# Tiles of the forgetting stage's output projection loaded piece by piece, and its residual tiles one unit ahead

## The chip, the core and the metric

The kernel runs on one core of one Trainium2 chip. The metric is the device time of one execution in microseconds; lower is better.

## The reference

One decoder layer on 1024 tokens of width 1024, in float32. What matters here is the middle of it, where two head groups are joined and projected, and the memory tokens are prepared for cross-attention:

```python
fx_out = forgetting_attention(fq, fk, fv, flf).reshape(B, S, FX_W)       # 8 heads of 64, causal, with decay
x = x + jnp.concatenate([ml_out, fx_out], axis=-1) @ w_out[l]            # ml_out: the mLSTM group, 4 heads of 128
x = x + cross_attention(rmsnorm(x, ln_x[l]), rmsnorm(mem, ln_mem[l]), w_xq[l], w_xkv[l], w_xo[l])
u = jax.nn.relu(rmsnorm(x, ln2[l]) @ w_ff1[l])
x = x + (u * u) @ w_ff2[l]
```

## The kernel before, in words

Every matrix product is taken as three products of a high and a low part (`mm3`, L182 to L184). The kernel goes through its stages one after another: input projections and mLSTM heads, forgetting attention, rest of the output projection, cross-attention, MLP. The change is in the forgetting stage.

That stage is a loop over slots. A slot (`slot`) takes one step of the softmax pipeline of forgetting attention: transposes of probabilities (L767), their cut into high and low parts (L130, L131), their product with the values (L786), scores of a later tile (L719, L720), row maximum (L726, L729), exponential (L741) and scaling on POOL (L752). Since the pipeline doesn't fill TensorE, each slot also takes a few matmul steps of other work, the filler (`filler`). The filler has 28 units in a fixed order: four groups of a key unit, a value unit and a key unit (keys and values of the memory tokens for cross-attention), then 16 output units (`out_unit(hf, n)`: half `hf` of the tokens, output tile `n`), which multiply the first five of the eight tiles of the joined heads ("mixes": four mLSTM heads and the first pair of forgetting heads) with `w_out_a`, add the residual tile x (L933), and store the sum (L934).

Inside a slot the order of each compute engine's instructions is fixed as written (`in_order`), and, from the first values on, that of the DMA issues on SP too. All DMAs are issued by SP, into one queue. So an ACT or DVE instruction of the filler that waits for a load holds back the attention work written behind it on that engine.

The filler's inputs come from memory in three ways. Its weights are loaded raw into one of two `wr` tiles (`raw_load`, L952) and cut into high and low halves on ACT (L965) and on POOL or DVE (L966), a few slots later (`cut_next`; at least `AGE` = 3 slots after the load). The mixes of one half are loaded at once by `mix_in(hf)`: `mix_load` issues two DMAs of four tiles (L850) and `mix_tile` two of one tile (L856). It is called for half 0 at the start of unit 10, and for half 1 inside `out_unit(0, 4)`. The residual tile is loaded at the start of its own unit (L925).

The outputs of key units, value units and the residual tiles use small tiles [128, 512], taken in turn by `rotate("p", "a")`: three buffers, two of tag p and one of tag a.

Of the kernel before, what the change touches and what calls it, by code (L numbers as in the profile page):

```python
# [9 lines left out]
F32 = mybir.dt.float32  # L10
F32R = mybir.dt.float32r
# [7 lines left out]
T = 1024  # L19
TH = 512  # L20
D = 1024
KT = D // P
NM = 256
MLH = 4
# [4 lines left out]
KX = 1  # L29
# [15 lines left out]
def hybrid_layer(ctx: ExitStack, tc: tile.TileContext, a: dict, out: bass.AP):  # L45
# [13 lines left out]
    def sb(tag, shape, bufs, dt=F32):  # L59
        return pool.tile(shape, dt, tag=tag, name=name(tag), bufs=bufs)  # L60

    def act(dt=F32R):
        return sb("act", [P, 8, TH], 7, dt)
# [12 lines left out]
    def z4():  # L76
        return sb("z4", [P, T + 3], 2)

    def w2(tag, n=512, dt=F32, p=P):
        return sb("r_" + tag, [P, 512], BUFS[tag], dt)[:p, :n]  # L80
# [30 lines left out]
    load = nc.sync.dma_start  # L111
# [47 lines left out]
    def rotate(*tags):  # L159

        spare[tags] = spare.get(tags, -1) + 1
        return w2(tags[spare[tags] % len(tags)])
# [23 lines left out]
    def both(pair, f):  # L186
        return f(pair[0]), f(pair[1])
# [107 lines left out]
    xs = [[t[:, k] for k in range(KT)] for t in (xa, xb)]  # L295
# [21 lines left out]
    for k in range(KT):  # L317
        if k == 2:
            load(wg_raw, a["w_gate"])
        if k % 2 == 0:  # L320
            c = slice(k % 4 * 256, k % 4 * 256 + 512)
# [39 lines left out]
    z, e, q, lf = (small[:, i:j].rearrange("p (t c) -> p t c", c=c) for i, j, c in ((0, 128, GC), (128, 224, GW), (224, 320, GW), (320, 416, GW)))  # L361
# [189 lines left out]
    mix = dram.tile([2, 2, P, KT, TH], F32, name="mix")  # L551
# [126 lines left out]
    for _ in range(2):  # L678
        t = act().rearrange("p a b -> p (a b)").rearrange("p (i c) -> p i c", i=4)
# [18 lines left out]
    def fx_step():  # L698
        if coming:
            dst, src = coming.pop(0)  # L700
            load(dst.bitcast(F32), src)
# [145 lines left out]
    def mix_load(k0, k1, hf):  # L847
        t = act().rearrange("p (e k) c -> p e k c", e=2)
        for p_ in range(2):
            load(t[:, p_, : k1 - k0].bitcast(F32), mix[hf, p_, :, k0:k1])  # L850
        return [(t[:, 0, k], t[:, 1, k]) for k in range(k1 - k0)]

    def mix_tile(k, hf):
        t = z4()[:, :T].bitcast(F32R).rearrange("p (e c) -> p e c", e=2)
        for p_ in range(2):
            load(t[:, p_].bitcast(F32), mix[hf, p_, :, k])  # L856
        return t[:, 0], t[:, 1]

    def out_proj(w_src, src, hf, sink):

        kn = len(src)
        per = w_src.shape[2] // (kn * P)
        for n in range(KT):
            if n % per == 0:
                w = both(weights(w_src[n // per], kn * per * P), lambda t: t.rearrange("p (k c) -> p k c", k=kn))
            at_ = n % per * P
            ps = mm()
            for k in range(kn):
                mm3(ps, both(w, lambda t: t[:, k, at_ : at_ + P]), src[k], k == 0, k == kn - 1)
            sink(n, hf, ps)  # L870


    late = []

    def void(_):
        return None

    def key_unit(n):
        def run(ws):
            w = both(ws[0], lambda t: t.rearrange("p (k c) -> p k c", k=KT))  # L880
            ps = mm()
            for k in range(KT):
                mm3(ps[:, :NM], both(w, lambda t: t[:, k]), (hm[:, 0, k], hm[:, 1, k]), k == 0, k == KT - 1)
                yield 1.5, k == KT - 1, lambda: sink(ps)

        def sink(ps):
            t = rotate("p", "a").rearrange("p (e c) -> p e c", e=2)
            v.tensor_tensor(out=t[:, 1], in0=ps[:, :NM], in1=row_m, op=ALU.mult)

            def store():  # L890
                split(t[:, 0].bitcast(F32R), t[:, 1].bitcast(F32R), t[:, 1])
                return lambda: void(load(kxd[n // 2, :, :, n % 2], t))

            return store

        return [a["w_xk"][n]], run

    def value_unit(hd):
        def run(ws):
            ws = [both(w, lambda t: t.rearrange("p (k c) -> p k c", k=4)) for w in ws]  # L900
            for t in range(2):
                ps = mm()[:, :NM]
                for k in range(KT):
                    x = (hm[:, 0, k, t * P : (t + 1) * P], hm[:, 1, k, t * P : (t + 1) * P])
                    mm3(ps, x, both(ws[k // 4], lambda z: z[:, k % 4]), k == 0, k == KT - 1)
                    yield 1.5, k == KT - 1, lambda: sink(t, ps)

        def sink(t, ps):
            o = rotate("p", "a").bitcast(F32R).rearrange("p (e c) -> p e c", e=2)
            split(o[:, 0], o[:, 1], ps, rcol_m[:, t : t + 1])  # L910
            return lambda: void(load(vxd[hd, :, :, t], o.bitcast(F32)))

        return [a["w_xv"][hd, i] for i in range(2)], run

    mixes = {}

    def mix_in(hf):
        mixes[hf] = mix_load(0, MLH, hf) + [mix_tile(k, hf) for k in range(MLH, MLH + KX)]

    def out_unit(hf, n):  # L920
        def run(ws):
            if n == 4 and hf == 0:
                mix_in(1)
            x = rotate("p", "a")
            load(x, a["x"][:, n, hf * TH : hf * TH + TH])  # L925
            w = both(ws[0], lambda t: t.rearrange("p (k c) -> p k c", k=MLH + KX))
            ps = mm()
            for k in range(MLH + KX):
                mm3(ps, both(w, lambda t: t[:, k]), mixes[hf][k], k == 0, k == MLH + KX - 1)
                yield 3.0, k == MLH + KX - 1, lambda: sink(x, ps)  # L930

        def sink(x, ps):
            v.tensor_tensor(out=x, in0=ps, in1=x, op=ALU.add)  # L933
            return lambda: void(load(x1d[hf, :, n], x))  # L934

        return [a["w_out_a"][n]], run

    units = []
# [45 lines left out]
    def filler():  # L984
        for u, (srcs, run) in enumerate(units):
            now[0] = u
            if u == len(units) - 2 * KT - 2:
                mix_in(0)
            while not now[2] and halves[0] < 2 * sum(w_ <= u for w_, _ in sources):
                yield None  # L990
            cut_for(u)
            yield from run(cuts_.pop(u))
# [8 lines left out]
    def slot(values, until):  # L1001
        with in_order((*COMPUTE, mybir.EngineType.SP) if values or until else COMPUTE):
            now[1] += 1
            todo_ = late[:]
            late.clear()
            closing = bool(ended)
            ended.clear()
            x = next(steps_, None) if values else None
            if x:
                x.turn()  # L1010

            while adds and not closing and len(adds) >= (LAG if x else 1):
                y = adds.pop(0)
                y.add()
                if y.last:
                    ended.append((y.hd, y.hf, y.ov))
                    break
            tops = scored[:]
            scored.clear()
            for t, e in tops:  # L1020
                t.top(e)
            if x:
                x.cut()
                adds.append(x)
            for hd, hf, ov in ended:
                fx_close(hd, hf, ov)
                if hd % 2:
                    stores.append((hd, hf, True))
            exps = topped[:]
            topped[:] = tops  # L1030
            for t, e in exps:
                t.exp(e)
            while exped:
                exped.pop(0).scale()
            exped.extend(t for t, e in exps if e == len(t.parts) - 1)
            fx_step()
            part = next(parts, None)
            if part:
                part[0].score(part[1])
                scored.append(part)  # L1040
            late.extend(filter(None, [f() for f in todo_]))
            if stores and stores[0][2]:
                stores[0] = (*stores[0][:2], False)
            elif stores:
                fx_store(*stores.pop(0)[:2])
            while spent[0] < until:
                step = next(fill, None)
                if step is None:
                    break
                spent[0] += step[0]  # L1050
                if step[1]:
                    late.append(step[2])
                    break
            if until and cut_next() and spent[0] + 6 < until:
                cut_next()
        return x
# [16 lines left out]
    n = 0  # L1073
# [4 lines left out]
    while adds or late or ended or stores:  # L1078
        n += 1
        slot(False, (n - DELAY) * RATE)  # L1080
# [233 lines left out]
    for n in range(KT):  # L1314
# [7 lines left out]
        k = n % 4  # L1322
# [128 lines left out]
    for at, (p_, i) in enumerate(jobs):  # L1451
# [14 lines left out]
        if i == 4:  # L1466
            b, k = todo[p_][:2]
# [48 lines left out]
    for at, (b, m) in enumerate(steps):  # L1516
# [10 lines left out]
        x = sums_of(m) if b == 0 else x2[m // 2][:, m % 2]  # L1527
# [22 lines left out]
    for i in range(2):  # L1550
        t = act()
# [123 lines left out]
```

## Time and profile before

| | us |
|---|---|
| median of 3 runs | 1533.2 (1532.7 to 1538.22) |
| the profiled execution's own time | 1537.44 |
| its span, first to last instruction | 1535.7 |
| TensorE matmuls busy in the span | 1504.1 |
| DVE, ACT, POOL busy | 1102.0, 731.7, 505.4 |

The time of an execution is a little longer than its span. A matmul's busy time overlaps that of the next one, so a busy TensorE is not yet one at its peak, but where it waits, the wait shows as a gap in its timeline. The forgetting stage's slots with value steps lie between about 392 and 612 us from the span's start.

### The profile page before, as it was taken

To read this page: it belongs to the slowest core of one execution; us is meant where nothing else is said; L and a number is where in the kernel's file an instruction comes from. 1 tells how busy PE (TensorE), PEld (TensorE's weight loads), DVE (VectorE), ACT (ScalarE), POOL (GpSimd) and SP (SyncE) were. 2 spreads that over 40 slices of the span, in tenths; PEclk is the share of its full clock that TensorE was granted. 3 is DMA by queue.
4 is the path that set the end of the run, shared out by engine and by line. 5 is a ranking of instruction groups with operands and counts; after the bars stand their busy time and mean duration, and the time that the engine had idled before them with its cause. 6 is when DMAs were issued, how large, how long until landed. Compare 5 with 4: busy or idle time off the path is not lost. (4 is left out here: it accounts for less than half of the span.)

```text
span 1535.7 us, 21948 instructions
## 1 busy us (share of the span) xinstructions
PE 1504.1 (98%) x7665; PEld 1260.2 (82%) x7665; DVE 1102.0 (72%) x1747; ACT 731.7 (48%) x1365; POOL 505.4 (33%) x543
## 2 busy tenths in 40 slices
PE   8999999999999999999999999999999999999997
PEld 8878888889998878788888877787787888888887
DVE  7656676764787776944557889888887567887665
ACT  7324343334686665644444457666665621121224
POOL 1002030413364442521110023554454365563322
PEclk9999999999999999999999999999999999999999
DMA  6422223435889786963344428777667777776623
GB/s 221 124 76 76 96 104 117 134 128 155 245 243 262 228 262 205 349 211 118 124 131 162 167 90 296 245 250 243 227 246 273 303 288 270 275 271 238 246 96 110
DMA packets 121530, 303.53 MB, mean 198 GB/s; under 512 B 13502, under 2 KB 28152, under 8 KB 113996
## 3 DMA queue, kind: packets, MB, share of 16 engines
q1 hardware_dynamic: 121420, 302.13, 58.2%
q8 instruction: 60, 0.98, 0.3%
q14 instruction: 50, 0.41, 0.1%
HBM read 202.22 MB, written 99.86 MB: 197 GB/s over the span
## 5 line engine op out<-in xcount | busy, mean ns | idle before, releaser
L182 PE MATMUL tp<-act,wl 128*128 128x512 f32 (+1 forms) x448 | 176.2, 393 | 1.8 <-DMA act<-mix 0.8
L183 PE MATMUL tp<-act,wh 128*128 128x512 f32 (+1 forms) x448 | 175.4, 391 | 0.0
L184 PE MATMUL tp<-act,wh 128*128 128x512 f32 (+1 forms) x448 | 175.0, 392 | 0.0
L131 DVE TENSOR_TENSOR wl<-wr,wh 128x1024 fp32r<-128x1024 f32 (+2 forms) x99 | 129.7, 1310 | 20.8 <-ACT wh L130 19.9
L130 ACT ACTIVATE wh<-wr 128x1024 fp32r<-128x1024 f32 (+2 forms) x99 | 98.9, 1000 | 84.0 <-PE tp L184 36.5
L182 PE MATMUL mm<-act,wl 128*128 128x512 f32 (+1 forms) x336 | 129.8, 386 | 0.9 <-DVE r_c L514 0.9
L183 PE MATMUL mm<-act,wh 128*128 128x512 f32 (+1 forms) x336 | 129.2, 385 | 0.0
L184 PE MATMUL mm<-act,wh 128*128 128x512 f32 (+1 forms) x336 | 128.9, 383 | 0.0
L182 PE MATMUL m<-act,wl 128*128 128x512 f32 (+1 forms) x312 | 119.7, 384 | 3.1 <-DVE wl L131 2.1
L184 PE MATMUL m<-act,wh 128*128 128x512 f32 (+1 forms) x312 | 119.7, 384 | 0.0
L183 PE MATMUL m<-act,wh 128*128 128x512 f32 (+1 forms) x312 | 119.3, 382 | 0.0
L182 PEld LDWEIGHTS tp<-act,wl 128*128 128x128 f32 x448 | 84.2, 188 | 21.7 <-ACT row L1368 1.2
L184 PEld LDWEIGHTS tp<-act,wh 128*128 128x128 f32 x448 | 84.2, 188 | 19.2
L183 PEld LDWEIGHTS tp<-act,wh 128*128 128x128 f32 x448 | 84.2, 188 | 18.9
L182 PE MATMUL sc<-act,wl 128*128 128x512 f32 (+1 forms) x248 | 97.0, 391 | 0.9 <-DVE wl L131 0.8
L183 PE MATMUL sc<-act,wh 128*128 128x512 f32 (+1 forms) x248 | 96.7, 390 | 0.0
L184 PE MATMUL sc<-act,wh 128*128 128x512 f32 (+1 forms) x248 | 96.7, 390 | 0.0
L130 ACT ACTIVATE wh<-z 128x1024 fp32r<-128x1024 f32 (+1 forms) x54 | 55.5, 1027 | 82.6 <-POOL z L1439 60.9
L1439 POOL TENSOR_TENSOR z<-wr 128x256 f32<-128x256 f32 x56 | 50.4, 921 | 133.7 <-DMA wr<-w_ff2q 126.3
L131 DVE TENSOR_TENSOR wl<-z,wh 128x1024 fp32r<-128x1024 f32 (+1 forms) x54 | 74.8, 1385 | 9.8 <-ACT wh L130 9.7
L130 ACT ACTIVATE w<-wr 128x768 fp32r<-128x768 f32 (+2 forms) x31 | 25.5, 824 | 105.0 <-PE tp L182 32.8
L182 PEld LDWEIGHTS mm<-act,wl 128*128 128x128 f32 x336 | 63.4, 189 | 13.8 <-DVE r_c L514 1.2
(683 smaller groups left out, 4254.8 us busy)
## 6 DMA issues: line engine op xcount, KB each, us to landing
act<-right SPq DMA_DIRECT2D x49, 1024.0 KB
right<-w SPq DMA_DIRECT2D x56, 256.0 KB
wr<-w_ff2q SPq DMA_DIRECT2D x28, 512.0 KB
right<-r_d SPq DMA_DIRECT2D x49, 256.0 KB
right<-r_e SPq DMA_DIRECT2D x49, 256.0 KB
act<-fqk SPq DMA_DIRECT2D x48, 256.0 KB
wr<-w_in SPq DMA_DIRECT2D x20, 512.0 KB
wr<-w_ff SPq DMA_DIRECT2D x20, 512.0 KB
```

The lines of the kernel that those rows point to most:

```text
L130: s.activation(hi, src, AF.Copy)
L131: return v.tensor_tensor(out=lo, in0=src, in1=hi.bitcast(F32), op=ALU.subtract)
L182: nc.tensor.matmul(ps, w[1], x[0], start=first, stop=False, skip_group_check=more)
L183: nc.tensor.matmul(ps, w[0], x[1], start=False, stop=False, skip_group_check=more)
L184: nc.tensor.matmul(ps, w[0], x[0], start=False, stop=last, skip_group_check=more)
L1439: g.tensor_tensor(out=o, in0=x, in1=y, op=op)
```

## The change

The mixes are no longer loaded by `mix_in` in one go. It allocates the tiles and puts ten pieces (five tiles, high and low) on a list; each slot issues one piece (`mix_step`, right behind the one load that the slot issues for the next attention head). For half 0 the list is made one unit earlier, at the start of unit 9. Whatever is left of a list is issued at the start of the first output unit of that half. Residual tiles are loaded one unit ahead (`x_in`), the first at the start of unit 11. The fillers' small tiles rotate among five buffers, `ROOM`: two of p, two of b, one of a.

```diff
-    def mix_tile(k, hf):
-        t = z4()[:, :T].bitcast(F32R).rearrange("p (e c) -> p e c", e=2)
-        for p_ in range(2):
-            load(t[:, p_].bitcast(F32), mix[hf, p_, :, k])
-        return t[:, 0], t[:, 1]
...
+    ROOM = ("p", "b", "p", "b", "a")
...
-            t = rotate("p", "a").rearrange("p (e c) -> p e c", e=2)
+            t = rotate(*ROOM).rearrange("p (e c) -> p e c", e=2)
...
     def mix_in(hf):
-        mixes[hf] = mix_load(0, MLH, hf) + [mix_tile(k, hf) for k in range(MLH, MLH + KX)]
+
+        t = act().rearrange("p (e k) c -> p e k c", e=2)
+        mixes[hf] = [(t[:, 0, k], t[:, 1, k]) for k in range(MLH)]
+        for _ in range(KX):
+            z = z4()[:, :T].bitcast(F32R).rearrange("p (e c) -> p e c", e=2)
+            mixes[hf].append((z[:, 0], z[:, 1]))
+        pieces.extend((mixes[hf][k][p_], mix[hf, p_, :, k]) for k in range(MLH + KX) for p_ in range(2))
+
+    def mix_step():
+        if pieces:
+            dst, src = pieces.pop(0)
+            load(dst.bitcast(F32), src)
+
+    def x_in(hf, n):
+        xs[hf, n] = rotate(*ROOM)
+        load(xs[hf, n], a["x"][:, n, hf * TH : hf * TH + TH])
 
     def out_unit(hf, n):
         def run(ws):
+            while n == 0 and pieces:
+                mix_step()
             if n == 4 and hf == 0:
                 mix_in(1)
-            x = rotate("p", "a")
-            load(x, a["x"][:, n, hf * TH : hf * TH + TH])
+            if hf == 0 or n + 1 < KT:
+                x_in(hf + (n + 1) // KT, (n + 1) % KT)
+            x = xs.pop((hf, n))
...
     def filler():
         for u, (srcs, run) in enumerate(units):
             now[0] = u
-            if u == len(units) - 2 * KT - 2:
+            if u == len(units) - 2 * KT - 3:
                 mix_in(0)
+            if u == len(units) - 2 * KT - 1:
+                x_in(0, 0)
...
             fx_step()
+            mix_step()
```

In the slots the compute engines keep their order: only buffer names differ there. What moves is the order on SP. Three places, each before and now. `act` and `z` with `mix` are the mixes, `fqk`, `decay` and `fvd` the next attention head's inputs, `wr` the filler's weights, `kxd` and `vxd` the stores of key and value units.

SP, around the load of half 0's mixes, up to the first weights of an output unit; before:

```order
L892 DMA kxd<-r_a_5017 256x1x256
L952 DMA wr_5096<-w_xk 128x1024
L701 DMA act_3178<-fqk 64x1024
L850 DMA act_5122<-mix 128x2048 x2
L856 DMA z_886_5125<-mix 128x512 x2
L701 DMA act_3178<-fqk 64x1024
L829 DMA w_896_5159<-fvd 128x1024
L701 DMA act_3178<-fqk 64x1024
L892 DMA kxd<-r_p_5120 256x1x256
L952 DMA wr_5182<-w_out_a 128x640
```

SP, the same place now; two more pieces stand just ahead of these rows, each behind an `fqk` load:

```order
L887 DMA kxd<-r_b_5017 256x1x256
L965 DMA wr_5100<-w_xk 128x1024
L701 DMA act_3178<-fqk 64x1024
L924 DMA act_5021<-mix 128x512
L701 DMA act_3178<-fqk 64x1024
L924 DMA act_5021<-mix 128x512
L829 DMA w_896_5159<-fvd 128x1024
L701 DMA act_3178<-fqk 64x1024
L924 DMA act_5021<-mix 128x512
L887 DMA kxd<-r_p_5125 256x1x256
L965 DMA wr_5183<-w_out_a 128x640
```

Before, all of half 0's mixes stand ahead of these weights; now five of the ten pieces do, and five stand behind.

SP, a few slots on, up to the third weights of an output unit; before:

```order
L803 DMA mix<-r_y_5276 128x512
L804 DMA mix<-r_f_4787 128x512
L911 DMA vxd<-r_p_5315 256x1x256
L952 DMA wr_5381<-w_out_a 128x640
L925 DMA r_p_5410<-x 128x512
```

SP, the same place now:

```order
L803 DMA mix<-r_y_5279 128x512
L804 DMA mix<-r_f_4787 128x512
L928 DMA r_p_5322<-x 128x512
L924 DMA z_861_5022<-mix 128x512
L906 DMA vxd<-r_a_5319 256x1x256
L924 DMA z_861_5022<-mix 128x512
L965 DMA wr_5389<-w_out_a 128x640
L928 DMA r_p_5418<-x 128x512
```

The last two pieces of half 0 and the first residual tile have come in here, ahead of the third weights.

SP, around the load of half 1's mixes; before:

```order
L952 DMA wr_5755<-w_out_a 128x640
L850 DMA act_5801<-mix 128x2048 x2
L856 DMA z_1046_5804<-mix 128x512 x2
L925 DMA r_p_5807<-x 128x512
L701 DMA act_3178<-fqk 64x1024
```

SP, the same place now:

```order
L965 DMA wr_5763<-w_out_a 128x640
L928 DMA r_b_5811<-x 128x512
L701 DMA act_3178<-fqk 64x1024
L924 DMA act_5809<-mix 128x512
L947 DMA x1d<-r_a_5614 128x512
L701 DMA act_3178<-fqk 64x1024
L924 DMA act_5809<-mix 128x512
```

The residual load (of the next unit now) stands ahead of half 1's first piece, where it stood behind all of its mixes.

Behind the slots, in the rest of the output projection and in cross-attention, the order is not fixed by the code but chosen by the scheduler at build time, and there some groups of matmuls have changed places on TensorE.

More of the change, by code (lines that the diff above doesn't have):

```diff
@@ L908, in sink @@
         def sink(t, ps):
-            o = rotate("p", "a").bitcast(F32R).rearrange("p (e c) -> p e c", e=2)
+            o = rotate(*ROOM).bitcast(F32R).rearrange("p (e c) -> p e c", e=2)
             split(o[:, 0], o[:, 1], ps, rcol_m[:, t : t + 1])
@@ L913, in value_unit @@
         return [a["w_xv"][hd, i] for i in range(2)], run
-    mixes = {}
+    mixes, pieces, xs = {}, [], {}
     def mix_in(hf):
-        mixes[hf] = mix_load(0, MLH, hf) + [mix_tile(k, hf) for k in range(MLH, MLH + KX)]
+        t = act().rearrange("p (e k) c -> p e k c", e=2)
[11 more added lines that the diff above has]
+        load(xs[hf, n], a["x"][:, n, hf * TH : hf * TH + TH])
     def out_unit(hf, n):
         def run(ws):
+            while n == 0 and pieces:
+                mix_step()
             if n == 4 and hf == 0:
                 mix_in(1)
-            x = rotate("p", "a")
-            load(x, a["x"][:, n, hf * TH : hf * TH + TH])
+            if hf == 0 or n + 1 < KT:
+                x_in(hf + (n + 1) // KT, (n + 1) % KT)
+            x = xs.pop((hf, n))
             w = both(ws[0], lambda t: t.rearrange("p (k c) -> p k c", k=MLH + KX))
```

## The prediction

> **What bounds the kernel now.** I read the page first, then TensorE's waits, then the timelines around the longest wait.
>
> ```profile
> span 1535.7 us, 21948 instructions
> PE 1504.1 (98%) x7665; PEld 1260.2 (82%) x7665; DVE 1102.0 (72%) x1747; ACT 731.7 (48%) x1365; POOL 505.4 (33%) x543
> ```
>
> TensorE is busy in 98% of the span and the other engines are not, so a change that leaves the matmuls alone can only win where TensorE stands still or runs slowly. TensorE's waits between 380 and 610 us, which is the forgetting stage (line waited for: total, times, longest):
>
> ```profile
> PE sc L719 <- ACT act L741: 4.6, 3, 3.2
> PE sc L719 <- ACT w L741: 1.5, 4, 0.5
> PE tp L767 <- DVE r_e L131: 1.1, 2, 0.9
> PE tp L767 <- DVE r_b L134: 0.5, 1, 0.5
> ```
>
> That is 7.7 us in all, 3.2 of it in one wait. TensorE's timeline around that wait, and ACT's:
>
> ```profile
> 496.54 0.39 PE L786 MATMUL ov<-r_d,w 128*128 128x512 f32 x1
> 500.17 0.80 PE L719 MATMUL sc<-act 128*128 128x512 f32 x1 [3.23 <-ACT act L741]
> 509.68 0.39 PE L182 MATMUL mm<-z,wl 128*128 128x512 f32 x1
> ...
> 493.06 0.48 ACT L133 ACTIVATE r_p<-mm,rcol_m 128x256 fp32r<-128x256 f32 x1
> 498.70 0.47 ACT L965 ACTIVATE wh<-wr 128x320 fp32r<-128x320 f32 x1 [5.16 <-DMA wr<-w_out_a]
> 499.56 0.47 ACT L741 ACTIVATE act<-sc,c_mx 128x256 f32<-128x256 f32 x1
> ...
> 501.58 0.47 ACT L965 ACTIVATE wh<-wr 128x320 fp32r<-128x320 f32 x1
> ```
>
> TensorE's scores need an exponential (L741); on ACT that stands behind the cut of the first `w_out_a` weights (L965), which waits 5.16 us for their load. So the load is what ends last. It costs more than the gap. In the windows view (length, busy us and count of PE, PEld, DVE, ACT, POOL, then granted clock, DMA share, GB/s):
>
> ```profile
> 473.90:498.70 24.80, 22.15 (x165) 20.42 (x163) 17.16 (x48) 15.99 (x42) 10.48 (x15) 1.00 0.95 281
> 500.20:506.10 5.90, 5.90 (x18) 5.03 (x19) 4.55 (x13) 3.34 (x11) 2.34 (x5) 0.50 0.55 185
> 545.40:546.70 1.30, 0.43 (x3) 0.04 (x1) 1.30 (x6) 0.14 (x1) 0.00 (x0) 1.00 1.00 239
> ```
>
> After the gap TensorE runs 5.9 us at a clock of 0.50, which loses another 2.95 us: 6.18 us for this one late load.
>
> Why it is late, SP's timeline and the sizes of its transfers show:
>
> ```profile
> 473.91 0.36 SPq L952 DMA_DIRECT2D wr<-w_xv  x1
> 474.31 1.13 SPq L701 DMA_DIRECT2D act<-fqk  x2
> 478.17 0.55 SPq L892 DMA_DIRECT2D kxd<-r_a  x1
> 479.00 0.38 SPq L952 DMA_DIRECT2D wr<-w_xk  x1
> 479.43 0.46 SPq L701 DMA_DIRECT2D act<-fqk  x1
> 479.94 1.06 SPq L850 DMA_DIRECT2D act<-mix  x2
> 481.04 1.33 SPq L856 DMA_DIRECT2D z<-mix  x2
> 482.42 1.16 SPq L701 DMA_DIRECT2D act<-fqk  x1
> 483.68 0.53 SPq L829 DMA_DIRECT2D w<-fvd  x1
> 484.26 0.45 SPq L701 DMA_DIRECT2D act<-fqk  x1
> 485.14 0.56 SPq L892 DMA_DIRECT2D kxd<-r_p  x1
> 487.37 0.34 SPq L952 DMA_DIRECT2D wr<-w_out_a  x1
> ...
> act<-fqk SPq DMA_DIRECT2D x48, 256.0 KB
> wr<-w_xv SPq DMA_DIRECT2D x8, 512.0 KB
> act<-mix SPq DMA_DIRECT2D x4, 1024.0 KB
> z<-mix SPq DMA_DIRECT2D x4, 256.0 KB
> w<-fvd SPq DMA_DIRECT2D x8, 512.0 KB
> wr<-w_out_a SPq DMA_DIRECT2D x16, 320.0 KB
> kxd<-r_a SPq DMA_DIRECT2D x4, 256.0 KB
> vxd<-r_a SPq DMA_DIRECT2D x4, 256.0 KB
> ```
>
> The weights are issued at 487.37 and land at 498.70, 11.3 us later. From 473.91 up to and with them SP issues 512 + 512 + 256 + 512 + 256 + 2048 + 512 + 256 + 512 + 256 + 256 + 320 = 6208 KB (w_xk has the shape of w_xv). At 24.79 us that is 250 KB a us; by the window's 281 GB/s, which also counts what was issued later, it is 274. The DMA engines' share there is 0.95: the queue is full, and 2560 KB of mixes, which no matmul can use before these weights are cut, stand ahead of weights that are needed at 493.54 (493.06 + 0.48), when ACT reaches them.
>
> **The change, part by part.** *Mixes in pieces, from one unit earlier.* A piece is 128x512, 256 KB. By the order on SP there now stand ahead of the first weights, counted from the same w_xv load and with them: 512 + 4 x 256 + 256 + 512 + 4 x 256 + 512 + 2 x 256 + 256 + 320 = 4928 KB, 1280 less. At 250 to 274 KB a us they land at 493.6 to 491.9. ACT would then wait 0.1 us or not at all; TensorE loses nothing as long as they land by 498.70 - 3.23 = 495.47. So gap and slow clock go: -6.18.
>
> What is late next: the bytes are the same, and without the gap TensorE asks for them sooner. The second weights are at 6280 KB, 499.0 to 496.8. Their cut stood at 501.58; without the gap and half of the 1.4 us at the slow clock up to there it comes at about 497.7, and with the same 1.9 us of slack (495.47 - 493.54) TensorE feels nothing before 499.6. The last `z` piece is the tight one: with the residual tile, five more pieces, the stores and the second weights ahead, it is at 8080 KB, and lands at 506.2 to 503.4. Its first matmul stood at 509.68 and now comes at 509.68 - 3.23 - 2.95 = 503.5. It is late by 0 to 2.7 us; nothing in the rows prefers an end, and I take the middle, +1.35. A wait of that length is under the 3.23 that went with the slow clock, so I add none for it.
>
> *Half 1's mixes and the residual tiles one unit ahead.* Before, the residual tile was queued behind 2560 KB of mixes; on DVE:
>
> ```profile
> DVE r_p L933 <- DMA r_p<-x: 9.6, 3, 4.4
> 545.11 0.69 DVE L933 TENSOR_TENSOR r_p<-mm,r_p 128x512 f32<-128x512 f32 x1 [4.45 <-DMA r_p<-x]
> ```
>
> DVE stands 9.6 us in three waits, and what is behind it on DVE, the cuts of L131, made TensorE wait 0.9 us right after the one at 545. Now that load stands ahead of the pieces and has a unit more of time: -0.9, and at least 0, since the pieces still share the queue with weights.
>
> *Five buffers.* A residual tile is loaded a unit earlier, so its buffer must be free sooner; five in turn instead of three give that, since a buffer comes round again five tiles later. No instruction is added on a compute engine: 0. Its price if that cover is gone is the DVE wait above, 4.45 us, of which TensorE felt 0.9.
>
> *Twelve more DMA issues on SP*, ten instead of four for each half. At the 0.3 to 0.6 us of the rows above they are 4 to 7 us of SP, spread over some 20 slots; SP waits for buffers there, and a load that is issued half a us later in a full queue lands no later. 0, at most one issue, 0.6, at the weights.
>
> *The scheduler's new order behind the slots.* The same matmuls in another order; no row of before shows their waits. Bounds: -1 to +1, about the largest single short wait above; I take 0.
>
> The sum against the profiled execution: 1537.44 - 6.18 + 1.35 - 0.9 = 1531.7, with 1.7 of it outside the span. The median of the runs is 4.2 below that execution. The same difference of 5.7 from it gives 1527.5.
>
> **The rivals.** *One: the slow clock is not in the median run.* The runs span 1532.7 to 1538.22, 5.5 us, with two at the low end, and the profiled one at the high end. The slow clock's 2.95 us are a part of that size. If only some runs have it, the median gains 3.23 - 1.35 + 0.9 = 2.8: 1530.4. Against it: the gap itself should be in every run, and 2.95 doesn't make 5.5. The Trainium skill (TensorE: Matmul & The Clock Gate, Part 1: The HAM clock gate) says that the gate judges activity in a free-running window of some 3.4 us and halves the clock after an idle one, so the same gap may or may not trip it; the trace agrees on the half, 0.50, but here a gap of 3.23 us, shorter than that window, was enough.
>
> *Two: more goes than the long wait.* The other waits of TensorE in the stage hang on ACT and DVE work that a late load can delay. If all 7.7 us and the 2.95 go, 10.65: 1522.6. For it speaks that weights and residual tiles all get a shorter queue; against it that most of the short waits name the pipeline's own work (L741, L131).
>
> *Three, slower: small pieces slow the queue.* Pieces are a quarter of the old transfers. If the queue falls to the lowest full-queue rate of the rows above, 239 GB/s (233 KB a us), the first weights still come in time (495.1), but the last `z` piece lands at 508.6, 5.1 us late. That is over 3.23, so the slow clock comes too: 8.05 in place of 6.18, +1.9. If half 1's ten pieces do the same where 0.9 was lost, +7.2 more: 1542.3. It decides from where the `z` wait reaches 3.23, at 506.7, 246 KB a us. Against it: the 250 were reached with two thirds of the bytes already in transfers of 256 to 512 KB. The Trainium skill speaks against the change here: DMA: Bandwidth & Descriptors, section Bandwidth, says to batch DMAs to 1 MiB or more for 75% of peak, and gives 341 GB/s at 1 MB and 138 at 64 KB; by an estimate halfway, 240, it would be this rival. The row's 281 with most transfers smaller than that does not bear it out for a queue with many in flight.
>
> *Four: nothing is won.* The weights would be late by the total of bytes and not by the mixes; the wait moves to the pieces: 1533.
>
> **How the numbers follow.** 0.5% of the time, 7.7 us, is about what a measurement of this kernel can tell from no change: under 1525.5 is faster, over 1540.9 slower. Forecast 0.40, with gains of 4 to 8.5 by the bounds (`z` 0 to 2.7, DVE 0 to 0.9, scheduler 1 either way), of which 0.06 lies past 7.7; rival one 0.18; two 0.22; three 0.16; four 0.04. Faster 0.06 + 0.22 = 0.28, slower 0.16, the rest 0.56. The range starts at rival two with a little scheduler, 1522, and ends at 1541, with about half of rival three outside.
>
> **What would show it.** Right: no gap of some 3 us on TensorE near 497, no stretch at clock 0.50 in the stage, ACT's L965 waiting under 1 us for w_out_a, DVE's L933 under 2 us for x, and TensorE's first matmul with `z` waiting 0 to 2.7 us. The first step is wrong if L965 still waits over 2 us for its first weights; the `z` term if a matmul there waits over 3. The forecast as a whole is wrong if the stage keeps a slow stretch, or if over 2 us move behind 612, where I put 0.

## The result, and the profile after

| | before | after |
|---|---|---|
| median of 13 runs, us | 1535.19 (1532.7 to 1538.68) | 1528.98 (1526.51 to 1532.35) |
| profiled execution's own time, us | 1537.44 | 1529.45 |
| its span, us | 1535.7 | 1527.5 |

The ratio is 0.9958, with a 95% interval of 0.995 to 0.9966: a little faster, by 6.2 us of the medians, under the 0.5% line. The median of before is now that of 13 runs, with the 3 that the prediction had among them. The profiled execution of before lies 2.25 above its median and that of after 0.47 above its own, so the two traces differ by 8.0 us in time (8.2 in span) where the medians differ by 6.2. Shares of the traces below add up to the 8, not to the 6.

The first lines of the page after, and TensorE's waits in the same stretch as before, 380 to 610 us (total, times, longest):

```profile
span 1527.5 us, 21949 instructions
PE 1500.2 (98%) x7665; PEld 1258.8 (82%) x7665; DVE 1105.8 (72%) x1747; ACT 732.6 (48%) x1365; POOL 507.7 (33%) x543
```

```profile
PE sc L719 <- ACT act L741: 1.5, 3, 1.0
PE sc L719 <- ACT w L741: 1.5, 4, 0.5
PE tp L182 <- DMA act<-mix: 1.0, 1, 1.0
PE tp L767 <- DVE r_b L134: 0.4, 1, 0.4
```

TensorE's wait for L741 has gone from 4.6 us (longest 3.2) to 1.5 (longest 1.0). Its wait for DVE's L131 (1.1) is gone. The 1.0 for `act<-mix` is at the end of the stage; before, it lay just outside the window. TensorE's timeline of after, at the place of the long wait, at the first matmul with `z`, and where DVE's late residual sum had held it at 546.66:

```profile
496.59 0.39 PE L786 MATMUL ov<-r_d,w 128*128 128x512 f32 x1
496.81 0.39 PE L719 MATMUL sc<-act 128*128 128x512 f32 x1
...
503.51 0.39 PE L182 MATMUL mm<-z,wl 128*128 128x512 f32 x1
...
539.45 0.60 PE L767 MATMUL tp<-ident,act 128*128 128x128 f32 x4
...
554.43 0.49 PE L767 MATMUL tp<-ident,w 128*128 128x128 f32 x3
...
603.36 0.47 PE L182 MATMUL tp<-act,wl 128*128 128x512 f32 x1 [1.03 <-DMA act<-mix]
```

The scores, which came at 500.17, come at 496.81 and don't wait. The first `z` matmul comes at 503.51, where the prediction's step put it (503.5) before it added a lateness, and doesn't wait either. The last three rows stood here before:

```profile
546.66 0.66 PE L767 MATMUL tp<-ident,act 128*128 128x128 f32 x4 [0.87 <-DVE r_e L131]
562.66 0.66 PE L767 MATMUL tp<-ident,w 128*128 128x128 f32 x4
611.38 0.47 PE L182 MATMUL tp<-act,wl 128*128 128x512 f32 x1 [0.77 <-DMA act<-mix]
```

So TensorE gains 3.4 us at the scores, 6.2 by 503.51, 7.2 by 539.45, 8.2 by 554.43 and 8.0 by the end of the stage. Behind it the two traces stay 7.5 to 9.7 apart, and 8.7 at the last group of matmuls.

ACT's timeline after, and SP's issues before it (the bracket is the wait and what ended it):

```profile
494.30 0.47 ACT L978 ACTIVATE wh<-wr 128x320 fp32r<-128x320 f32 x1 [0.71 <-DMA wr<-w_out_a]
495.16 0.47 ACT L741 ACTIVATE act<-sc,c_mx 128x256 f32<-128x256 f32 x1
498.13 0.47 ACT L978 ACTIVATE wh<-wr 128x320 fp32r<-128x320 f32 x1 [0.41 <-DMA wr<-w_out_a]
```

```profile
473.90 0.36 SPq L965 DMA_DIRECT2D wr<-w_xv  x1
...
482.76 0.47 SPq L924 DMA_DIRECT2D act<-mix  x1
484.87 0.56 SPq L887 DMA_DIRECT2D kxd<-r_p  x1
485.91 0.33 SPq L965 DMA_DIRECT2D wr<-w_out_a  x1
...
498.23 0.65 SPq L924 DMA_DIRECT2D z<-mix  x1
```

The first weights land at 494.30, 8.4 us after their issue, where they took 11.3. The cut waits 0.71 us in place of 5.16, and the exponential behind it is done before TensorE asks. In the windows view (columns as in the prediction) the queue moves more than before, 294 GB/s where it was 281, and behind it the clock is 1.00:

```profile
473.90:498.70 24.80, 23.91 (x178) 22.37 (x177) 20.27 (x56) 19.70 (x53) 11.74 (x17) 1.00 1.00 294
498.70:512.00 13.30, 13.30 (x74) 11.27 (x73) 10.77 (x32) 9.66 (x30) 8.28 (x15) 1.00 1.01 298
```

### The profile page after: what moved, and what is told of

Read it like the earlier page. It is cut to its first block, busy times and chain, and to the rows that moved or that the text cites. A ratio compares the mean times of both kernels' runs of the same rounds, so it can differ in the third digit from the quotient of the medians.

```text
span 1527.5 us, 21949 instructions
## 1 busy us (share of the span) xinstructions
PE 1500.2 (98%) x7665; PEld 1258.8 (82%) x7665; DVE 1105.8 (72%) x1747; ACT 732.6 (48%) x1365; POOL 507.7 (33%) x543
## 5 line engine op out<-in xcount | busy, mean ns | idle before, releaser
L131 DVE TENSOR_TENSOR wl<-wr,wh 128x1024 fp32r<-128x1024 f32 (+2 forms) x99 | 128.4, 1297 | 22.5 <-ACT wh L130 21.7
L131 DVE TENSOR_TENSOR wl<-z,wh 128x1024 fp32r<-128x1024 f32 (+1 forms) x54 | 74.5, 1379 | 8.6 <-ACT wh L130 8.4
```

What stands on the lines that cost most here:

```text
L131: return v.tensor_tensor(out=lo, in0=src, in1=hi.bitcast(F32), op=ALU.subtract)
```

## The experiments

The theory is that the time comes from the KB that SP queues ahead of the first `w_out_a` weights. The rivals are that the spreading itself does it, that the residual tiles and buffers do it, and that an earlier load does it whatever its shape. Diffs are against the changed kernel unless said otherwise, and ratios are against before on the same chip.

The traces don't reach this place at the same time. A score matmul ahead of it stands at 479.74 us before and 479.75 after, but 0.2 us earlier with half 0's pieces alone, 0.5 with the mixes whole one unit earlier, 0.7 with the residual tiles alone, 0.8 with all pieces and no residual tiles ahead, and 1.2 in the second profile of before. Positions below are as the traces have them.

**Half 0's pieces alone.** Half 1's mixes are loaded whole, and the residual tiles at their own unit in three buffers:

```diff
-    ROOM = ("p", "b", "p", "b", "a")
+    ROOM = ("p", "a")
...
+        if hf == 1:
+            pieces.clear()
+            for p_ in range(2):
+                load(t[:, p_].bitcast(F32), mix[hf, p_, :, 0:MLH])
...
-            if hf == 0 or n + 1 < KT:
-                x_in(hf + (n + 1) // KT, (n + 1) % KT)
+            x_in(hf, n)
...
-            if u == len(units) - 2 * KT - 1:
-                x_in(0, 0)
```

> Only half 0's mixes are loaded in pieces (from unit 9 on); half 1's mixes in one go inside out_unit(0, 4), residual tiles at their own unit and three buffers, as before. Theory Q (the first w_out_a weights were late because of the KB queued ahead of them): they land at about 494, the wait of 3.2 us near 497 and the slow clock go, TensorE is 6 us earlier by 510; the waits at 545 and 560 (about 2 us together) stay. About -6 us, ratio 0.996. Rival P (the buffers and late residual tiles held the SP queue and so the weights): the wait near 497 stays, ratio 1.000. Rival S (the scheduler's new order behind the slots gave the gain): no change up to 600 us, what changes comes behind.

Measured: 1530.65 us, ratio 0.9981 (0.9964 to 0.9999; its runs scattered more than the others'). ACT's timeline, and TensorE's at the end of the stage:

```profile
494.43 0.47 ACT L984 ACTIVATE wh<-wr 128x320 fp32r<-128x320 f32 x1 [1.09 <-DMA wr<-w_out_a]
```

```profile
603.49 0.47 PE L182 MATMUL tp<-act,wl 128*128 128x512 f32 x1 [1.39 <-DMA act<-mix]
```

The gap and the slow clock are gone, and the matmul at 603.49 is within 0.3 us of the changed kernel's, at 603.36, when the 0.2 from ahead of the place is counted. So in the trace this part alone brings the gain of the stage. TensorE's waits at 545 and 560, which were expected to stay, are gone too, though DVE still waits for `x`. Its times fit anything between 0.2 and 5.5 us.

**Residual tiles ahead and five buffers alone.** Both halves' mixes are loaded whole again, and half 0's at unit 10, as before:

```diff
+        if True:
+            pieces.clear()
+            for p_ in range(2):
+                load(t[:, p_].bitcast(F32), mix[hf, p_, :, 0:MLH])
...
-            if u == len(units) - 2 * KT - 3:
+            if u == len(units) - 2 * KT - 2:
```

> Only the residual tiles a unit ahead and the five buffers; both halves' mixes in one go at the old places. Theory Q: the wait of 3.2 us near 497 and the slow clock stay; DVE's waits for x (9.6 us) go, and with them TensorE's at 545 and 560: -1 to -2 us, ratio 0.999. Rival P: the wait near 497 goes too, ratio 0.996.

Measured: 1533.03 us, ratio 0.999 (0.9978 to 1.0002). The gap stays. TensorE's timeline, and the windows ahead of the gap and behind it:

```profile
499.47 0.80 PE L719 MATMUL sc<-act 128*128 128x512 f32 x1 [3.17 <-ACT act L741]
```

```profile
473.90:498.70 24.80, 21.49 (x160) 19.77 (x159) 16.52 (x46) 16.02 (x43) 10.62 (x16) 1.00 0.98 296
499.30:502.70 3.40, 3.23 (x12) 2.95 (x13) 2.78 (x8) 2.33 (x9) 0.88 (x2) 0.50 0.84 299
502.70:506.00 3.30, 3.30 (x18) 2.76 (x17) 2.56 (x8) 2.17 (x9) 1.65 (x5) 1.00 0.39 112
```

The slow stretch is half as long here, and the matmul that stood at 506.22 comes 1.9 us earlier. No DVE instruction waits for `x` any more, and TensorE is 3.0 us ahead at the transposes that stood at 546.66 and 4.0 at those of 562.66. So in the trace the part is worth 2.1 us by itself, a shorter slow stretch apart. By the interval of the times it is anything from a loss of 0.3 to a gain of 3.4.

**The mixes whole, one unit earlier**, built on the kernel before:

```diff
-            if u == len(units) - 2 * KT - 2:
+            if u == len(units) - 2 * KT - 3:
```

> The kernel before with one edit: half 0's mixes, still in one go, are issued one unit earlier (unit 9). Theory Q: the same 6208 KB stand ahead of the first w_out_a weights, so they come at 495.5 to 498.7 (250 to 287 KB a us) and the wait near 497 shrinks to between 0 and 3 us; but the last w_xk weights, cut on ACT at 484.8, now stand behind all mixes (4352 KB from 473.9) and land at 489 to 491: a new wait of 4 to 6 us on ACT, 2 to 4 on TensorE. No gain: ratio 0.998 to 1.002. Rival (the head start alone is enough): ratio 0.996, no wait over 1 us near 485 or 497.

Measured: 1535.09 us, ratio 0.9999 (0.9988 to 1.001). The waits of ACT and DVE (total, times, longest), TensorE's timeline, and a window:

```profile
ACT wh L965 <- DMA wr<-w_xk: 4.1, 1, 4.1
ACT wh L965 <- DMA wr<-w_out_a: 1.9, 2, 1.1
...
DVE r_p L933 <- DMA r_p<-x: 7.9, 3, 6.0
```

```profile
543.70 0.66 PE L767 MATMUL tp<-ident,act 128*128 128x128 f32 x4 [2.40 <-DVE r_e L131]
```

```profile
544.30:547.70 3.40, 3.40 (x11) 2.72 (x10) 2.84 (x9) 2.40 (x6) 1.14 (x3) 0.50 0.87 244
```

The gap at 497 is gone here as well, but the wait moves. The `w_xk` weights, issued one unit ahead of the `w_out_a` weights, are 4.1 us late now, and TensorE is 1.7 behind by 491. It has won 4.4 us by the matmul that stood at 505.88. Then a residual tile is 6.0 us late, which gives a gap of 2.40 and a slow stretch at 544, and 1.1 us, with the 0.5 from ahead of the place in it, is left at the last group of matmuls. An earlier start without the pieces relieves one load at the cost of another.

**Larger pieces.** Five of 512 KB in place of ten of 256, one a slot, so that all 2560 KB are issued ahead of the first weights:

```diff
-        pieces.extend((mixes[hf][k][p_], mix[hf, p_, :, k]) for k in range(MLH + KX) for p_ in range(2))
+        for k in range(MLH):
+            pieces.append((t[:, :, k], mix[hf, :, :, k].rearrange("e p c -> p e c")))
...
```

> The changed kernel with five pieces of 512 KB (high and low part of a tile in one DMA) instead of ten of 256 KB, one per slot as before. All five now stand ahead of the first w_out_a weights: 6208 KB as in the kernel before, but the same w_xk place as in the changed kernel. Theory Q (KB ahead in the queue): the weights come 3 to 4 us later than in the changed kernel, at 495.5 to 498; ACT waits 2 to 4 us there, TensorE 0 to 2.5 us; -4 to -6 us against before, ratio 0.996 to 0.9975. Rival (it is the size of a DMA or the spreading over slots that counts): ACT's wait stays under 1 us, ratio 0.9955.

Measured: 1536.24 us, ratio 0.9998 (0.9987 to 1.0009). ACT's and TensorE's timelines, and the window:

```profile
500.04 0.47 ACT L981 ACTIVATE wh<-wr 128x320 fp32r<-128x320 f32 x1 [6.49 <-DMA wr<-w_out_a]
```

```profile
501.51 0.80 PE L719 MATMUL sc<-act 128*128 128x512 f32 x1 [4.55 <-ACT act L741]
```

```profile
473.90:498.70 24.80, 21.98 (x162) 20.00 (x160) 16.67 (x48) 15.41 (x41) 10.55 (x15) 1.00 1.02 270
```

All that was won is lost again, more than I had expected. The loads are spread over slots here as well. What differs is that 6208 KB stand ahead of the weights again. The queue also has more ahead of the `w_xk` weights, whose cut waits 2.3 us, and the `w_out_a` weights are issued at 488.32, 2.4 us later than after. This run decides between the theory and the spreading as such. A handicap of the size of 512 KB isn't excluded by it, but the window's 270 GB/s, beside 265 with 128 KB, gives it no support.

**Smaller pieces.** Twenty of 128 KB, two a slot, so that the KB ahead stay as in the changed kernel:

```diff
-        pieces.extend((mixes[hf][k][p_], mix[hf, p_, :, k]) for k in range(MLH + KX) for p_ in range(2))
+        for k in range(MLH + KX):
+            for p_ in range(2):
+                for c in range(0, TH, TH // 2):
+                    pieces.append((mixes[hf][k][p_][:, c : c + TH // 2], mix[hf, p_, :, k, c : c + TH // 2]))
...
             mix_step()
+            mix_step()
```

> The changed kernel with twenty pieces of 128 KB (half a row of 512 each, 1 KB a partition), two per slot, so that the same KB stand at the same places. Theory Q: time as the changed kernel within 0.5 us, ratio 0.9955 to 0.996; ACT's first wait for w_out_a about 1 us. Rival three of the prediction (small pieces slow the queue): fewer KB a us between 474 and 505, ACT waits over 2 us for w_out_a, TensorE over 1 us at its first matmul with the z tile; ratio 0.997 to 1.000.

Measured: 1529.98 us, ratio 0.9956 (0.9942 to 0.9971), not to be told from the changed kernel. In the trace the signs of the prediction's rival three show all the same. Windows, ACT's and TensorE's timelines:

```profile
473.90:498.70 24.80, 22.95 (x171) 21.14 (x170) 18.13 (x51) 18.37 (x50) 11.38 (x16) 1.00 1.03 265
```

```profile
495.69 0.47 ACT L981 ACTIVATE wh<-wr 128x320 fp32r<-128x320 f32 x1 [2.90 <-DMA wr<-w_out_a]
```

```profile
497.16 0.50 PE L719 MATMUL sc<-act 128*128 128x512 f32 x1 [0.97 <-ACT act L741]
506.07 0.47 PE L183 MATMUL mm<-z,wh 128*128 128x512 f32 x1 [1.71 <-DMA z<-mix]
```

There are 265 GB/s, a gap of 0.97, and a `z` piece 1.71 us late. No slow clock follows. One trace doesn't show that the size did it, since the window's rate with 256 KB pieces was anything from 269 to 294 GB/s in the eight traces that have them.

**Pieces one unit later**, as late as the whole load was:

```diff
-            if u == len(units) - 2 * KT - 3:
+            if u == len(units) - 2 * KT - 2:
```

> The changed kernel, but half 0's pieces start at unit 10, as the whole load did before; the pieces left over are issued together at the first output unit. Theory Q: only two pieces stand ahead of the first w_out_a weights, so these are early and the wait near 497 goes; the last z piece stands a few places later in the queue than in the changed kernel and lands at 503 to 507, needed at 503.5: a wait of 0 to 3 us on TensorE there. Ratio 0.995 to 0.998. Rival (the unit's head start is what does it): the weights still wait, ratio 0.999 to 1.000.

Measured: 1529.23 us, ratio 0.9963 (0.9948 to 0.9978). The weights land at 493.65 (ACT waits 0.28), but on TensorE the mixes are the late ones:

```profile
502.33 0.50 PE L182 MATMUL mm<-act,wl 128*128 128x512 f32 x1 [0.46 <-DMA act<-mix]
503.81 0.50 PE L183 MATMUL mm<-act,wh 128*128 128x512 f32 x1 [0.98 <-DMA act<-mix]
```

That is 1.4 us. The lateness that the prediction feared for `z` appears when the pieces start one unit later. With the earlier start and 256 KB pieces no matmul there waits for its mixes in any of seven traces, though the times can't tell the two kernels apart.

**All pieces, no residual tiles ahead.** Three buffers, and the residual tile loaded at its own unit:

```diff
-    ROOM = ("p", "b", "p", "b", "a")
+    ROOM = ("p", "a")
...
-            if hf == 0 or n + 1 < KT:
-                x_in(hf + (n + 1) // KT, (n + 1) % KT)
+            x_in(hf, n)
...
-            if u == len(units) - 2 * KT - 1:
-                x_in(0, 0)
```

> The changed kernel without its second half: mixes of both halves in pieces, but residual tiles loaded at their own unit and the three buffers of before. Theory Q: no large load stands ahead of a residual tile any more, DVE waits for x under 3 us in all and TensorE not at 540 or 553; same as the changed kernel within 0.5 us, ratio 0.9955 to 0.9962. Rival P (the residual tiles' head start and the buffers are worth what TensorE lost at 545 and 560): +1 to +2 us, ratio 0.9965 to 0.997.

Measured: 1531.06 us, ratio 0.9963 (0.9949 to 0.9977). DVE's timeline, and TensorE's at the end of the stage:

```profile
524.16 0.69 DVE L945 TENSOR_TENSOR r_p<-mm,r_p 128x512 f32<-128x512 f32 x1 [3.88 <-DMA r_p<-x]
553.08 0.69 DVE L945 TENSOR_TENSOR r_p<-mm,r_p 128x512 f32<-128x512 f32 x1 [3.03 <-DMA r_p<-x]
```

```profile
605.58 0.47 PE L182 MATMUL tp<-act,wl 128*128 128x512 f32 x1 [1.13 <-DMA act<-mix]
```

The residual tiles are late again, by 6.9 us in these two waits where under 3 in all were expected, and TensorE is 2.2 us behind the changed kernel at the same matmul, although it was 0.8 ahead at 479. The earlier residual load pays once half 1's mixes come in pieces. The times alone would not show it.

**Half 0's pieces and the residual tiles ahead; half 1 whole.**

```diff
+        if hf == 1:
+            pieces.clear()
+            for p_ in range(2):
+                load(t[:, p_].bitcast(F32), mix[hf, p_, :, 0:MLH])
...
```

> Half 0's mixes in pieces, residual tiles a unit ahead, five buffers; half 1's mixes in one go inside out_unit(0, 4), as before the change. If the pieces of half 1 are worth nothing by themselves (the run with half 0's pieces alone had no more TensorE waits up to 600 than the changed kernel): within 1 us of the changed kernel, ratio 0.9955 to 0.9965, no wait over 1 us near 540. If the pieces of half 1 do spare weights a wait: +1 to +2 us on the changed kernel, ratio 0.9965 to 0.997.

Measured: 1528.82 us, ratio 0.9951 (0.9939 to 0.9964). The changed kernel, run beside it on the same chip, gave 1527.77:

> The changed kernel as it is, timed on the same chip as the run above, to set that one against: ratio 0.995 to 0.9966, no slow clock in the forgetting stage.

Its ratio was 0.995 (0.9936 to 0.9964). The two can't be told apart, and with half 1 whole the matmul at 603.36 stands at 603.28. Half 1's pieces are worth nothing that can be seen in the stage. Behind it, on TensorE and in a window, something else shows that is used below:

```profile
641.73 0.50 PE L182 MATMUL mm<-act,wl 128*128 128x512 f32 x1 [1.76 <-DVE wl L131]
```

```profile
642.20:645.60 3.40, 3.40 (x10) 2.61 (x9) 3.40 (x4) 2.46 (x4) 2.33 (x2) 0.50 0.88 240
```

**Four buffers** in place of five:

```diff
-    ROOM = ("p", "b", "p", "b", "a")
+    ROOM = ("p", "b")
```

> The changed kernel with four small buffers in turn (two of p, two of b) instead of five. A buffer then comes round four tiles later, still after its store. No wait for x on DVE, no new wait on TensorE; within 0.5 us of the changed kernel, ratio 0.9953 to 0.9963. If the fifth buffer is needed: SP waits for stores ahead of the residual loads, weights behind them come late, +1 us or more.

Measured: 1529.95 us, ratio 0.9957 (0.9943 to 0.997). No DVE instruction waits for `x`. TensorE has a gap of 0.45 near 497 and waits 1.73 for `act<-mix` at the end of the stage, where no new wait was expected, but the time doesn't show it. The fifth buffer is worth nothing that can be measured; three with the residual tiles ahead weren't tried.

**The other three tiles in pieces, too.** TensorE's last wait in the stage, 1.0 us for `act<-mix`, hangs on the loads of `mix_load` for the rest of the projection, so these were split by tile as well:

```diff
-            load(t[:, p_, : k1 - k0].bitcast(F32), mix[hf, p_, :, k0:k1])
+            for k in range(k0, k1):
+                load(t[:, p_, k - k0].bitcast(F32), mix[hf, p_, :, k])
```

> The changed kernel with one more edit behind the slots: the last three tiles of the joined heads (mix_load) are loaded tile by tile, so that only the last tile's load waits for the last heads' store. Theory: TensorE's wait of 1.0 us for act<-mix at 602 goes or falls under 0.5; ratio 0.995 to 0.9957. Rival: the first tile's load is issued no sooner, since SP is in order there too, and nothing changes: 0.9958.

Measured: 1531.83 us, ratio 0.9968 (0.9956 to 0.9981): no gain. The wait at 603 goes, but the scheduler's order behind the slots changes with it. TensorE's timeline and a window:

```profile
629.04 1.05 PE L230 MATMUL ov<-ones,r_b 128*128 128x1 f32 x8 [2.55 <-POOL r_b L222]
```

```profile
630.90:634.30 3.40, 3.40 (x9) 2.61 (x9) 3.02 (x7) 2.99 (x5) 1.56 (x2) 0.50 0.89 281
```

One microsecond is saved, 2.55 are lost in a wait for POOL and some more in a slow stretch. No version tried is measurably better than the changed kernel.

**The kernel before again**, one profile, for the slow clock:

> The kernel before as it is, one more profile. If the slow clock belongs to the gap and only its length depends on the moment: a gap of 3.2 us near 497 again, followed by 3.4 or 6.8 us at half clock. If rival one is right that some executions go without: the gap, and no stretch at half clock in the stage.

Measured: 1536.54 us. TensorE's timeline and the window behind the gap; below them the same window of the first profile of before:

```profile
500.33 0.79 PE L719 MATMUL sc<-act 128*128 128x512 f32 x1 [4.63 <-ACT act L741]
```

```profile
498.70:505.50 6.80, 5.17 (x16) 4.49 (x17) 4.53 (x12) 4.86 (x15) 3.20 (x6) 0.50 0.64 221
```

```profile
499.30:506.13 6.83, 5.96 (x18) 5.10 (x19) 5.06 (x13) 4.24 (x14) 3.21 (x6) 0.50 0.61 213
```

Gap and slow clock are there again, the slow stretch as long as the first time.

**All runs in one table.** For the first `w_out_a` weights: KB issued from the `w_xv` load up to and with them, time from that load's issue to the cut, ACT's wait at the cut, and TensorE's gap at L719, all read from the timelines of SP, ACT and TensorE:

| kernel | KB ahead | us | ACT wait | gap |
|---|---|---|---|---|
| before | 6208 | 24.8 | 5.16 | 3.23 |
| before again | 6208 | 26.2 | 6.55 | 4.63 |
| residual tiles ahead alone | 6208 | 24.8 | 5.09 | 3.17 |
| 512 KB pieces | 6208 | 26.6 | 6.49 | 4.55 |
| whole, one unit earlier | 6208 | 23.0 | 1.14 | 0 |
| 128 KB pieces | 4928 | 22.5 | 2.90 | 0.97 |
| four buffers | 4928 | 22.0 | 2.37 | 0.45 |
| other three tiles in pieces | 4928 | 21.9 | 2.27 | 0.36 |
| all pieces, no residual tiles ahead | 4928 | 21.9 | 2.20 | 0.29 |
| after again | 4928 | 21.0 | 1.40 | 0 |
| half 0's pieces and residual tiles | 4928 | 20.8 | 1.18 | 0 |
| half 0's pieces alone | 4928 | 20.7 | 1.09 | 0 |
| after | 4928 | 20.4 | 0.71 | 0 |
| pieces one unit later | 4160 | 20.0 | 0.28 | 0 |

The gap is the wait less 1.93 us in every row, to 0.02, and nothing where the wait is shorter. With 1280 KB less the weights come 2.3 to 6.2 us sooner where the mixes are loaded from the same or a similar slot on. Three things show that the KB are not all. With the whole mixes a unit earlier the weights come in 23.0 us though the KB ahead are the same; one reading is that the 2560 KB then follow the `w_xv` load at once, and the window from 473.9 to 498.7 has 319 GB/s there, the most of all. Among the rows with 4928 KB the time still varies from 20.4 to 22.5 us. And the last 768 KB, in the last row, bring only 0.4.

## Why the prediction was right, step by step

**The gap and its slow clock, -6.18.** Held. TensorE had gained 6.2 us by 503.51. That half 0's mixes ahead of the weights set it, and not the spreading as such, is shown by half 0's pieces alone, by the residual tiles alone and by the 512 KB pieces together. The whole load one unit earlier takes this wait away too, but gives most of its gain back. The slack of TensorE behind the cut, worked out as 495.47 - 493.54 = 1.93, is the 1.93 of the table. The sign that ACT waits under 1 us for these weights holds in the profile of after (0.71), but not in the second one (1.40), and four variants with the same 4928 KB ahead wait 2.20 to 2.90 us and keep a gap of 0.29 to 0.97. So the long gap and its slow clock are gone in every trace with 4928 KB or less, but the wait isn't gone in all of them. The landing was 0.7 us later than the late end of the forecast: 491.9 to 493.6 against 494.30, which is 241 KB a us by the in-order count where the sum had at least 250. The slack hid that. Why the count falls short, in the table's last row most of all, isn't settled. A queue whose later transfers share the engines with earlier ones would do it; no run separates that.

**The second weights, no effect.** Held: 0.41 us of ACT's wait, none on TensorE.

**The last `z` piece, +1.35.** Mis-sized: 0. The queue moved 294 and 298 GB/s in the two windows above, 287 and 291 KB a us, more than the 250 to 274 from which the term came, and the first `z` matmul didn't wait. The range of 0 to 2.7 was right in its low end, and I had no row to prefer it by. It isn't far off: a `z` piece was 1.71 us late with 128 KB pieces, and `act` pieces 1.4 with pieces one unit later. That a wait under 3.23 would bring no slow clock, as the term had it, was wrong: gaps of 2.40 and 2.55 did in other runs, so the upper end of its range was too cheap.

**Half 1 and the residual tiles, -0.9.** Mis-sized in the trace: -2.0, 1.0 between 503.51 and 539.45 and 1.0 more by 554.43. I had priced the 0.87 at 546.66 alone. The second 1.0 comes in short waits around another late residual tile, on DVE's timeline of before:

```profile
559.24 0.69 DVE L933 TENSOR_TENSOR r_p<-mm,r_p 128x512 f32<-128x512 f32 x1 [2.76 <-DMA r_p<-x]
```

After, no DVE instruction waits there. The residual tiles alone give the same 2.1, so that part can carry it; half 0's pieces alone also reach the place at 603, with DVE still waiting for `x`. These two relieve the same waits and don't add. Only with half 1 in pieces are the residual tiles ahead needed, and there they are worth 2.2 in the trace.

**Five buffers and twelve more issues on SP, 0.** Held for the buffers, by the four-buffer run. For the issues no experiment isolates the price; the weights were issued 1.5 us earlier than before, not later.

**The scheduler behind the slots, 0 within 1.** Held for this kernel: 8.2 us at 554.4 and 8.7 at the last group of matmuls, with swings of 1 us either way between. The run with the other three tiles in pieces shows that it was no safe term: there the new order cost a wait of 2.55.

**The sum.** The two wrong terms are off by 1.35 and 1.1 in the same direction. Against the profiled execution, which moved by 8.0, the forecast of -5.7 is short by 2.3. The median moved by 6.2, since the trace of before was a long run by 2.25 and that of after by 0.47. That the forecast of the median, 1527.5, came out near the measured 1528.98 is therefore in part luck, and the medians can't be split by terms. One sum of the prediction doesn't come out of its own bounds: a gain of 6.18, with 0 to 2.7 off for `z`, 0 to 0.9 added and 1 either way, lies between 2.5 and 8.1 us, and not between 4 and 8.5. The 8.0 of the traces is at the edge of it.

**The rivals.** One, a slow clock in some runs only: it is in both profiles of before and in that of the residual tiles alone, but with half its length in the latter. The mean granted clock of each run speaks against it too: 6.8 us at half clock take 0.002 off the mean of a run, and of 60 runs of before on the three chips (one of 3823 us left out) 57 have 0.995 to 0.997, where the 13 of after have 0.997 or 0.998 (of the 5 of its second timing one has 0.996). The mean also holds a slow stretch at the end of the kernel, so it doesn't sort every run. Three runs of before have 0.998, with 1531.2 to 1532.7 us, so a few may go without. The runs' scatter, which had suggested the rival, is mostly not from there: after, with no slow stretch in its two profiles, still spans 5.8 us. Two, more than the long wait, came halfway in the trace: 8.2 us by 554.43, between the 6.18 of the one wait and the 10.65 of all. Three is refuted for 256 KB: the queue moved 269 to 294 GB/s there, never near the 239 of the rival, and no `z` matmul waited; at 128 KB a late `z` piece shows, which the size need not have caused. Four is refuted by the result.

## What to carry to other kernels

When a cut waits for a load, count the KB that its queue was given ahead of it, and ask which of them are needed later than the load itself: moving 1280 KB behind it was worth the whole gap, or all but 1 us of it, while the same loads spread over slots, with all KB still ahead, were worth nothing. Price a late load by the slack of the engine that matters (here ACT's wait less 1.93 us), and where that comes to 2.4 us or more, add the slow clock behind it, as all six such gaps between matmuls here had it; of the waits from 1.71 to 1.93 us one in six had it. Don't add up the gains of parts that relieve the same waits; one run with one part alone tells which one carries them.

## What the runs showed of the hardware

The clock of 0.50 came in two lengths. It lasted 6.83 us behind gaps of 3.23, 4.63 and 4.55 us, and 3.4 behind gaps of 3.17, 2.40 and 2.55; with half 1 whole and the residual tiles ahead, also behind a single wait of 1.76 at 642. So 3.17 and 3.23 us at the same place cost 3.4 and 6.83 us of slow clock. The window of the 512 KB pieces behind their gap, and two waits without a slow clock behind them (the mixes whole one unit earlier; the residual tiles alone, with the window behind that wait):

```profile
499.50:506.30 6.80, 4.79 (x15) 4.19 (x16) 4.15 (x11) 4.85 (x15) 3.13 (x6) 0.50 0.86 289
...
491.13 0.39 PE L719 MATMUL sc<-act 128*128 128x256 f32 x1 [1.93 <-ACT act L741]
...
645.70 0.50 PE L182 MATMUL mm<-act,wl 128*128 128x512 f32 x1 [1.76 <-DVE wl L131]
645.70:649.10 3.40, 3.40 (x15) 2.77 (x16) 3.40 (x3) 2.55 (x5) 2.60 (x2) 1.00 0.75 220
```

Waits of 1.93 and 1.76 brought none there, nor did 1.75 and 1.71 with 128 KB pieces and 1.73 with four buffers. So around 1.8 us the length of a wait doesn't decide it.

Nor does the length of the gap decide how long the slow clock lasts. The windows shown order it in another way: in the three long stretches TensorE still stands for 0.87, 1.63 and 2.01 us (busy 5.96 of 6.83, 5.17 of 6.80, 4.79 of 6.80), in the four short ones for 0.17 us or not at all (3.23 and three times 3.40 of 3.40). In these seven, then, the stretch doubles where the gap reaches well into it; no run was made to test that.

The Trainium skill (TensorE: Matmul & The Clock Gate, Part 1: The HAM clock gate) gives a free-running window of 3413 ns; the two lengths agree with one and two of these. It also lets the clock fall after an idle window of about 3.4 us. The waits of 2.40, 2.55 and 1.76 us here were shorter and were enough.

The size of a transfer alone did not set the rate of the queue between 473.9 and 498.7 us. With whole mixes it was 281 and 286 GB/s in the two profiles of before, 296 with the residual tiles alone and 319 with the mixes one unit earlier; it was 269 to 294 in the eight kernels with 256 KB pieces, 270 with 512 KB and 265 with 128 KB. The ranges overlap, and a small loss with small pieces is neither shown nor excluded. The Trainium skill's rule is to batch DMAs to 1 MiB or more (DMA: Bandwidth & Descriptors, Bandwidth). A loss as large as the prediction's rival took from it, to 240 GB/s, doesn't show here for a queue with this many transfers in flight.
